# Moving element-wise work between GpSimd, VectorE and ScalarE in a two-layer trunk kernel: GpSimd keeps short powers and copies

## The chip, the cores and the metric

The kernel runs on one core of a Trainium2 chip. The metric is the device time of one execution in microseconds (us), here the median of three runs. Five engines take part, each with its own queue that it works off in order: TensorE (PE in the rows; PEld is its loading of weights), VectorE (DVE), ScalarE (ACT), GpSimd (POOL), and SyncE (SP), which here only issues transfers (DMA).

## The reference

A trunk of two layers runs on 512 new tokens and, with the same weights, on 8 single tokens of running sequences, so the kernel has 520 columns. Each layer is a mixer and a gated feed-forward network (FFN), each behind an RMS norm and with a residual sum. The first mixer multiplies chunks of 128 positions by a triangular matrix. The second is a gated delta rule, which is where most of the change lies. Cut to it:

```python
q, k, v = split(silu(short_conv(proj, w_conv)))      # 4 taps, per channel
q = l2norm(q) * DK ** -0.5;  k = l2norm(k)
beta = sigmoid(b_raw);  g = -exp(a_log) * softplus(a_raw + dt_bias)
gc = cumsum(g)                                        # within a chunk
decay = where(i >= j, exp(gc[i] - gc[j]), 0)
L = where(i > j, (k * beta) @ k.T * decay, 0)
Tm = inverse(I + L)
u, w = Tm @ (v * beta),  Tm @ (k * beta * exp(gc))
A = (q @ k.T) * decay
for each chunk:                                       # the scan
    v_new = u - w @ S
    o = (q * exp(gc)) @ S + A @ v_new
    S = S * exp(g_last) + (k * exp(g_last - gc)).T @ v_new
out = (rmsnorm(o) * silu(gate)) @ w_out
```

The kernel takes chunks of 128 positions in place of the reference's 64 for this rule: there are 8 heads of 128 and 4 chunks, 32 blocks of 128x128 in all.

## The kernel before, in words

Everything is kept with channels on the 128 partitions and the 520 columns along the free dimension, in two halves of 256 and 264 columns. Each projection is a row of tiles of weights, 128 output channels by 1024 input channels. A tile comes by DMA (`load_raw`), ScalarE rounds it to the type that TensorE multiplies fast (`split_w`, the CAST on L145), and VectorE or GpSimd takes the difference between the tile and its rounded form, its *rest* (L146). `mm3` then multiplies a half by three products (rounded by rounded, and rounded by rest both ways): 24 matmuls a half (L176), or 8 pairs of wider ones in the FFNs and the first mixer (L181, L182). A pool of three buffers each holds raw tiles and split tiles.

Stages, in the times of the profile: first mixer up to about 313 us, FFN 0 to 690, the delta layer to about 1103, FFN 1 to 1484, then the final norm. Within the delta layer: the end of FFN 0 and the norm in front of it (690 to 712); gates per position and the eight key tiles (712 to 815); the inverse of the 32x32 diagonal blocks on VectorE, beside which TensorE does projections (815 to 868); then the merging of these blocks, query and value tiles, the scan over chunks, and the output projection (868 to 1103).

A key tile (`key_tile`, L632) is a `conv_tile` (two `mm3`, scaled by L596; first tap on ScalarE L599, three taps on VectorE L601, the 8 single columns L602, Silu on ScalarE L603), and then two steps that `after(n, step)` puts off until n further `mm3` have been issued. `normalise` transposes the tile on TensorE (L642), squares it on ScalarE (L645), adds the epsilon (L646), takes `rsqrt`, and scales (L648). `back` transposes the result (L653) and makes the form scaled by decay (L655). TensorE works in order too, so a `back` that is not ready holds up all matmuls behind it.

`rsqrt` (L114) is nine small VectorE instructions (L121 to L130): a bit trick and two polynomial steps. The norms of the trunk (`Norm.add`, `Norm.factors`, `Norm.finish`) add squares into `sqacc` (L213, GpSimd unless told otherwise), sum over partitions on TensorE (L222), take `rsqrt`, and spread it over all partitions on TensorE (L244).

`decay` (L577) loads a row of cumulated decay for a head to all partitions, masks it on GpSimd (L580) and subtracts on VectorE (L581); one Exp over 16 blocks follows on ScalarE (L678). `lower` multiplies the key products by it (L669). `scan_step` (L817) does one chunk for four heads; it has two PSUM banks by turns, one of which (`po`) takes the output of the chunk.

The order on each engine comes from a scheduler with its own costs, except where `pin` and `after` fix it; so an edit can move instructions far from it.

Of the kernel before, what the change touches and what calls it, by code (L numbers as in the profile page):

```python
# [15 lines left out]
P = 128  # L16
# [5 lines left out]
H = 8  # L22
# [16 lines left out]
def trunk(  # L39
# [11 lines left out]
    wraw = ctx.enter_context(tc.tile_pool(name="wraw", bufs=3))  # L51
    wspl = ctx.enter_context(tc.tile_pool(name="wspl", bufs=3))
# [49 lines left out]
    G.memset(ones, 1.0)  # L102
    warm = cst.tile([P, 1], F32, name="warm")
# [90 lines left out]
    class Norm:  # L194
# [7 lines left out]
        def add(self, x, k, h, eng=None, split=False):  # L202
# [4 lines left out]
            else:  # L207
# [5 lines left out]
                (eng or G).tensor_tensor(a, a, t, ALU.add)  # L213
# [76 lines left out]
    def out_proj(w_out, k0, nk, act, x, xin=None, then=None, early=((), ()), halves=(0, 1), tail=2):  # L290
        ws, first = dict(early[0]), dict(early[1])
        order = [(j, h) for h in range(2) for j in ws] + [(n, h) for n in range(len(ws), 8 - tail) for h in range(2)]
        for j, h in order + [(j, h) for h in halves for j in range(8 - tail, 8)]:
            if j not in ws:
                ws[j] = weights(w_out[j][:, k0:k0 + nk, :], nk, G if then and j >= 6 else V)
# [63 lines left out]
    for u in range(8):  # L359
        ws = [weights(a_w_in[16 + 2 * u + j], eng=G if u == 1 else V) if u else w0[j] for j in range(2)]  # L360
# [77 lines left out]
    def ffn(layer, x, feed, then):  # L438
        w_in, w_out = f_w_in[layer], f_w_out[layer]
        hf, norm = feed.act, feed.norm  # L440
        for c0f, nk in ((0, 8), (8, 8), (16, 6)):
            mid = act_pair(3, "fm")
            for k in range(nk):
                wg = weights(w_in[c0f + k], eng=G if c0f + k == 0 else V)
# [7 lines left out]
                wu = weights(w_in[NF + c0f + k], eng=G if c0f + k == 0 else V)  # L452
# [21 lines left out]
    ffn(0, x, feed, feed_b)  # L474
    wide[0] = False
    hb, norm = feed_b.act, feed_b.norm


    gate_d = tc.dram_tile([P, H, TT], F32, name="gate_d")
    rows_d = tc.dram_tile([96, C], F32, name="rows_d")  # L480
    smp_d = tc.dram_tile([NS, 3, H], F32, name="smp_d")
    dl_d = tc.dram_tile([H, NS, P], F32, name="dl_d")

# [19 lines left out]

    order = [8 + i for i in range(8)] + [24 + i for i in range(5)] + [0, 1, 2, 3, 16, 17, 18, 19, 4, 5, 6, 7, 20, 21, 22, 23, 29, 30, 31]
    ready = {}
    POOL_LO = 17

    def stream(n):
        i = order.index(n)
        for j in order[i:i + 2]:  # L510
            if j not in ready:
                ready[j] = weights(b_w_in[j], eng=G if i < POOL_LO else V)
# [39 lines left out]
    V.tensor_copy(gc, ps[:, 0:32])  # L552
    egl = cst.tile([P, H, NCH], F32, name="egl")
# [23 lines left out]
    def decay(t, hd, keep, sign, base):  # L577
# [3 lines left out]
        V.tensor_tensor(t4, t4, gc[:, 4 * hd:4 * hd + 4, None].to_broadcast((P, 4, C)), ALU.subtract)  # L581
# [8 lines left out]
    def conv_tile(w, n, dst, y=None):  # L590
# [9 lines left out]
        for j in range(1, 4):  # L600
            V.scalar_tensor_tensor(y[:, :T], raw[:, j:j + T], wc[:, n, j:j + 1], y[:, :T], ALU.mult, ALU.add)  # L601
        V.scalar_tensor_tensor(y[:, T:TT], raw[:, 515:523], wc[:, n, 3:4], cs[:, n, :], ALU.mult, ALU.add)  # L602
# [29 lines left out]
    def key_tile(hd):  # L632
# [17 lines left out]
        def back():  # L650
# [4 lines left out]
            G.tensor_tensor(kt[:, q0:q0 + 4], kn, kdec[:, q0:q0 + 4, None].to_broadcast((P, NCH, C)), ALU.mult)  # L655
# [6 lines left out]
    def lower(hd):  # L662
# [5 lines left out]
        for c in range(NCH):  # L668
            V.scalar_tensor_tensor(L[:, q0 + c, :], ps[:, c * C:(c + 1) * C], beta[:, hd, c:c + 1], L[:, q0 + c, :], ALU.mult, ALU.mult)  # L669

    for hd in range(H):
# [4 lines left out]
        if hd in (2, 4):  # L676
            half = L[:, 8 * hd - 16:8 * hd]
            S.activation(half, half, AF.Exp, scale=-1.0)  # L678
# [95 lines left out]
    for gr in range(2):  # L774
        half = AT[:, 16 * gr:16 * gr + 16]
        S.activation(half, half, AF.Exp)

    def query_post(hd):
# [14 lines left out]
        G.tensor_tensor(qc[:, :T], qc[:, :T], er, ALU.mult)  # L793
# [23 lines left out]
    def scan_step(gr, c):  # L817
# [6 lines left out]
        if c:  # L824
# [9 lines left out]
            G.tensor_tensor(S4, S4, egl[:, hs, c:c + 1].to_broadcast((P, 4, P)), ALU.mult)  # L834
# [301 lines left out]
```

## Time and profile before

| | |
|---|---|
| time, median of 3 runs | 1494.62 us (1493.44 to 1494.76) |
| profiled execution | 1499.04 us; span of the trace 1497.3 us |
| granted TensorE clock, mean | 0.984 of full speed |
| busy in the span | PE 1442.0 us (96%), PEld 1359.5, DVE 888.3 (59%), ACT 584.4 (39%), POOL 436.9 (29%) |
| chain of work that ended last | PE 83%, DVE 11%, ACT 2%, issue 2%, DMA 1% |

The profiled execution lies 4.4 us above the median. Busy shares are means over the whole span: TensorE is busy almost throughout, and the stretches in which it is not are looked up by time. A wait of TensorE is shown with the instruction whose end released it.

### The profile page before, as it was taken

How to read it: one execution, taken by the hardware profiler on the slowest of the kernel's cores; microseconds unless marked ns; L12 is line 12 of the kernel's file. 1: busy time of each engine (PE TensorE's matmuls, PEld its weight loads, DVE VectorE, ACT ScalarE, POOL GpSimd, SP SyncE). 2: the span in 40 equal slices, each digit the busy share in tenths (PEclk: the TensorE clock that was granted, in tenths of full speed). 3: DMA queues.
4: the chain of work that ended last, by engine and by line, in shares of the span. 5: the costliest groups of instructions: out<-in, count | busy, mean ns of one | idle time of the engine just before them, and what ended most of it. 6: DMA issues, size and time to landing. Idle time of an engine off the chain costs nothing.

```text
span 1497.3 us, 27192 instructions
## 1 busy us (share of the span) xinstructions
PE 1442.0 (96%) x10752; PEld 1359.5 (91%) x10752; DVE 888.3 (59%) x1911; ACT 584.4 (39%) x1187; POOL 436.9 (29%) x468
## 2 busy tenths in 40 slices
PE   8999999999999999998788899999999999999997
PEld 7999999989999999997788888999999999999997
DVE  7657546664444444457787988676764454454454
ACT  6545324543313331333643255433533313331333
POOL 1113102333302320336444212311234412430333
PEclk9999999999999999999899999999999999999999
DMA  6222232322333333234312224334523553444332
GB/s 200 85 87 87 80 91 85 98 85 85 99 88 96 93 91 98 87 90 137 103 58 72 84 75 129 86 99 138 168 77 114 139 151 117 123 145 132 118 96 68
DMA packets 79359, 155.54 MB, mean 104 GB/s; under 512 B 10848, under 2 KB 41216, under 8 KB 79232
## 3 DMA queue, kind: packets, MB, share of 16 engines
q1 hardware_dynamic: 78944, 153.27, 33.9%
q8 instruction: 85, 1.39, 0.4%
q10 hardware_dynamic: 288, 0.52, 0.1%
q14 instruction: 42, 0.34, 0.1%
HBM read 142.18 MB, written 11.59 MB: 103 GB/s over the span
## 4 chain that ended last, share of the span: by engine, by line
PE 83%; DVE 11%; ACT 2%; issue 2%; DMA 1%; POOL 0%; SPq 0%; ACTq 0%; DVEq 0%; POOLq 0%
PE mm L176 42%; PE mm L181 22%; PE mm L182 11%; DVE r L601 1%; DVE inv L702 1%; PE ax L426 1%; PE ax L890 1%; DVE t L601 1%; DVE sc L701 1%; DMA raw<-in_a_w_in 1%; DVE rs_u L125 1%; PE ax L354 1%; DVE L L581 1%; DVE inv L694 1%; PE sx L842 1%
## 5 line engine op out<-in xcount | busy, mean ns | idle before, releaser
L145 ACT CAST wsp<-raw 128x1024 fp32r<-128x1024 f32 (+2 forms) x225 | 231.4, 1029 | 356.3 <-PE mm L176 298.5
L146 DVE TENSOR_TENSOR wsp<-raw,wsp 128x1024 fp32r<-128x1024 f32 (+2 forms) x193 | 235.2, 1219 | 87.8 <-ACT wsp L145 86.8
L176 PE MATMUL mm<-hf,wsp 128*128 128x264 f32 x2112 | 270.6, 284 | 0.0
L176 PEld LDWEIGHTS mm<-hf,wsp 128*128 128x128 f32 x2112 | 261.7, 188 | 3.7
L181 PE MATMUL mm<-hf,wsp 128*128 128x512 f32 x704 | 251.9, 397 | 0.0
L176 PE MATMUL mm<-hb,wsp 128*128 128x256 f32 (+1 forms) x1536 | 210.4, 293 | 6.8 <-DVE t L596 4.6
L176 PEld LDWEIGHTS mm<-hb,wsp 128*128 128x128 f32 x1536 | 196.2, 196 | 8.5 <-DVE t L596 3.8
L182 PE MATMUL mm<-hf,wsp 128*128 128x256 f32 x704 | 197.6, 281 | 0.0
L450 POOL TENSOR_TENSOR t<-t,rbc 128x256 f32<-128x256 f32 x88 | 95.1, 1081 | 314.1 <-ACT t L449 314.1
L181 PEld LDWEIGHTS mm<-hf,wsp 128*128 128x128 f32 x704 | 133.1, 189 | 27.9
L192 POOL TENSOR_TENSOR fm<-t,fm 128x256 fp32r<-128x256 f32 x88 | 95.9, 1090 | 147.6 <-ACT fm L191 147.6
L176 PE MATMUL mm<-fm,wsp 128*128 128x264 f32 x1056 | 135.2, 285 | 0.0
L182 PEld LDWEIGHTS mm<-hf,wsp 128*128 128x128 f32 x704 | 133.0, 189 | 0.0
L176 PEld LDWEIGHTS mm<-fm,wsp 128*128 128x128 f32 x1056 | 131.3, 190 | 1.6
L181 PE MATMUL mm<-fm,wsp 128*128 128x512 f32 x352 | 125.2, 395 | 0.0
L255 DVE TENSOR_TENSOR t<-mm,rbc 128x264 f32<-128x264 f32 (+1 forms) x160 | 68.2, 428 | 93.5 <-PE mm L176 90.4
L299 DVE TENSOR_TENSOR x<-mm,x 128x264 f32<-128x264 f32 (+1 forms) x128 | 54.5, 426 | 102.2 <-PE mm L176 73.3
L186 DVE TENSOR_TENSOR mm<-mm,t 128x256 f32<-128x256 f32 x120 | 51.7, 432 | 103.4 <-ACT t L185 103.2
L185 ACT COPY t<-mm 128x256 f32<-128x256 f32 x120 | 44.7, 373 | 142.6 <-PE mm L182 140.3
L181 PE MATMUL mm<-hn,wsp 128*128 128x512 f32 x256 | 96.1, 410 | 3.2 <-DVE hn L278 2.0
L176 PE MATMUL mm<-hn,wsp 128*128 128x264 f32 x768 | 99.2, 286 | 0.0
L182 PE MATMUL mm<-fm,wsp 128*128 128x256 f32 x352 | 98.6, 280 | 0.0
(331 smaller groups left out, 2233.3 us busy)
## 6 DMA issues: line engine op xcount, KB each, us to landing
raw<-in_f_w_in SPq DMA_DIRECT2D x88, 512.0 KB, 3.6
raw<-in_f_w_out SPq DMA_DIRECT2D x32, 512.0 KB, 3.6
raw<-in_b_w_in SPq DMA_DIRECT2D x32, 512.0 KB, 3.6
raw<-in_a_w_in SPq DMA_DIRECT2D x31, 512.0 KB, 3.6
raw<-in_a_w_out SPq DMA_DIRECT2D x16, 512.0 KB, 3.7
raw<-in_f_w_out SPq DMA_DIRECT2D x16, 384.0 KB, 3.1
L<-rows_d SPq DMA_DIRECT2D x16, 256.0 KB, 3.6
t<-in_st_delta SPq DMA_DIRECT2D x16, 256.0 KB, 3.2
```

The costliest lines, as they stand in the source:

```text
L145: S.copy(hi, r)
L146: (eng or V).tensor_tensor(w[:, 1, i:i + n, :], r, hi.bitcast(F32), ALU.subtract)
L176: PE.matmul(ps[:, :n], lhsT=w[:, a, k, :], rhs=act[:, b, k, c0:c0 + n], start=k + a + b == 0, stop=k == nk - 1 and a == 1)
L181: PE.matmul(ps.rearrange("p (b t) -> p b t", b=2), lhsT=w[:, 0, k, :], rhs=act[:, :, k, c0:c0 + n], start=k == 0, stop=last, skip_group_ch ...
L182: PE.matmul(ps[:, :n], lhsT=w[:, 1, k, :], rhs=act[:, 0, k, c0:c0 + n], start=False, stop=last, skip_group_check=True)
L185: S.copy(b, ps[:, n:])
L186: V.tensor_tensor(ps[:, :n], ps[:, :n], b, ALU.add)
L192: (eng or G).tensor_tensor(act[:, 1, k, c0:c0 + n], tmp, hi.bitcast(F32), ALU.subtract)
L255: V.tensor_tensor(t, ps[:, :n], self.r[:, c0:c0 + n], ALU.mult)
L299: V.tensor_tensor(dst, ps[:, :w], (xin(j)[:, c0:c0 + w] if xin else dst), ALU.add)
L450: G.tensor_tensor(s, s, norm.r[:, c0:c0 + nn], ALU.mult)
L601: V.scalar_tensor_tensor(y[:, :T], raw[:, j:j + T], wc[:, n, j:j + 1], y[:, :T], ALU.mult, ALU.add)
```

## The change

1. `rsqrt` of up to 4 columns becomes one GpSimd instruction, a `pow` with exponent -0.5. It serves the ten half norms of the trunk, the norm of `v` in the first mixer, the eight key tiles and the eight scan steps.
2. Rests of weights (L146) are all taken by VectorE; GpSimd had 28 tiles of 128x1024 and four of 128x768. The pools of raw and split tiles get a fourth buffer.
3. The norm's adds (L213) go from GpSimd to VectorE.
4. The subtraction in `decay` goes; in its place each of the 64 blocks has its own Exp on ScalarE with a bias per partition. The bias for `L` contains the logarithm of beta, so that `lower` is one product per head where it was four.
5. In `conv_tile` the 8 single columns ride on the last tap, after a ScalarE copy.
6. The scaling of keys (L655) and of the state (L834) go from GpSimd to ScalarE, in pieces of 128x128; the scaling of queries (L793) and of the scan's output (L859) go from GpSimd to VectorE. The scan's output is no longer copied from PSUM first (L850): squares and final product read PSUM.
7. Small loads and products for the running sequences' convolution (L484 to L502) are issued ahead of FFN 0.

```diff
-    wraw = ctx.enter_context(tc.tile_pool(name="wraw", bufs=3))
-    wspl = ctx.enter_context(tc.tile_pool(name="wspl", bufs=3))
+    wraw = ctx.enter_context(tc.tile_pool(name="wraw", bufs=4))
+    wspl = ctx.enter_context(tc.tile_pool(name="wspl", bufs=4))
...
     def rsqrt(s, n, p=P):
+        if n <= 4:
+            y = sm.tile([P, 4], F32, tag="rs_p", name=nm("rs_p"), bufs=4)[:p, :n]
+            G.tensor_tensor(y, s, mhalf[:p].to_broadcast((p, n)), ALU.pow)
+            return y
...
-                (eng or G).tensor_tensor(a, a, t, ALU.add)
+                (eng or V).tensor_tensor(a, a, t, ALU.add)
...
-                ws[j] = weights(w_out[j][:, k0:k0 + nk, :], nk, G if then and j >= 6 else V)
+                ws[j] = weights(w_out[j][:, k0:k0 + nk, :], nk)
...
-        ws = [weights(a_w_in[16 + 2 * u + j], eng=G if u == 1 else V) if u else w0[j] for j in range(2)]
+        ws = [weights(a_w_in[16 + 2 * u + j], eng=V) if u else w0[j] for j in range(2)]
...
-                ready[j] = weights(b_w_in[j], eng=G if i < POOL_LO else V)
+                ready[j] = weights(b_w_in[j], eng=V)
...
+    lnb = small([P, H, 5], "lnb")
+    S.activation(lnb, beta, AF.Ln)
     V.reciprocal(beta, beta)
+    V.tensor_scalar(lnb, lnb, -1.0, -BIG, ALU.mult, ALU.max)
...
+    gcb = cst.tile([P, 32], F32, name="gcb")
+    V.tensor_tensor(gcb.rearrange("p (h c) -> p h c", c=4), gc.rearrange("p (h c) -> p h c", c=4), lnb[:, :, 0:4], ALU.add)
+    ngc = cst.tile([P, 32], F32, name="ngc")
+    V.tensor_scalar(ngc, gc, -1.0, None, ALU.mult)
...
-        V.tensor_tensor(t4, t4, gc[:, 4 * hd:4 * hd + 4, None].to_broadcast((P, 4, C)), ALU.subtract)
+
+    def decay_exp(t, q0, sign, bias):
+        for q in range(q0, q0 + 16):
+            S.activation(t[:, q], t[:, q], AF.Exp, bias=bias[:, q:q + 1], scale=sign)
...
-        for j in range(1, 4):
-            V.scalar_tensor_tensor(y[:, :T], raw[:, j:j + T], wc[:, n, j:j + 1], y[:, :T], ALU.mult, ALU.add)
-        V.scalar_tensor_tensor(y[:, T:TT], raw[:, 515:523], wc[:, n, 3:4], cs[:, n, :], ALU.mult, ALU.add)
+        S.copy(y[:, T:TT], cs[:, n, :])
+        for j, m in ((1, T), (2, T), (3, TT)):
+            V.scalar_tensor_tensor(y[:, :m], raw[:, j:j + m], wc[:, n, j:j + 1], y[:, :m], ALU.mult, ALU.add)
...
-            G.tensor_tensor(kt[:, q0:q0 + 4], kn, kdec[:, q0:q0 + 4, None].to_broadcast((P, NCH, C)), ALU.mult)
+            for c in range(NCH):
+                S.activation(kt[:, q0 + c], kn[:, c], AF.Copy, scale=kdec[:, q0 + c:q0 + c + 1])
...
-        for c in range(NCH):
-            V.scalar_tensor_tensor(L[:, q0 + c, :], ps[:, c * C:(c + 1) * C], beta[:, hd, c:c + 1], L[:, q0 + c, :], ALU.mult, ALU.mult)
+        V.tensor_tensor(L[:, q0:q0 + 4], lanes(ps), L[:, q0:q0 + 4], ALU.mult)
...
-            half = L[:, 8 * hd - 16:8 * hd]
-            S.activation(half, half, AF.Exp, scale=-1.0)
+            decay_exp(L, 8 * hd - 16, -1.0, gcb)
...
-        half = AT[:, 16 * gr:16 * gr + 16]
-        S.activation(half, half, AF.Exp)
+        decay_exp(AT, 16 * gr, 1.0, ngc)
...
-        G.tensor_tensor(qc[:, :T], qc[:, :T], er, ALU.mult)
+        V.tensor_tensor(qc[:, :T], qc[:, :T], er, ALU.mult)
...
-            G.tensor_tensor(S4, S4, egl[:, hs, c:c + 1].to_broadcast((P, 4, P)), ALU.mult)
+            for i, hd in heads:
+                S.activation(Sd[:, hd], Sd[:, hd], AF.Copy, scale=egl[:, hd, c:c + 1])
...
-        S.copy(o_c, lanes(po))
...
-            S.activation(jk[:, i], o_c[:, i, :], AF.Square, accum_out=so[:, i:i + 1])
+            S.activation(jk[:, i], po[:, i * P:(i + 1) * P], AF.Square, accum_out=so[:, i:i + 1])
...
-        (V if gr and c == 3 else G).tensor_tensor(o_c, o_c, ro[:, :, None].to_broadcast((P, 4, P)), ALU.mult)
+        V.tensor_tensor(o_c, lanes(po), ro[:, :, None].to_broadcast((P, 4, P)), ALU.mult)
...
-        fin.add(x, k, h, G if h else V, split=True)
+        fin.add(x, k, h, V, split=True)
```

The order of instructions changes with it. The lines below carry each program's own line numbers; the changed program's are higher by 6 at the weights and by 14 to 16 in the delta layer (L146 becomes L152, L645 becomes L661, L648 becomes L664, L603 becomes L619, L701 and L702 become L716 and L717).

On VectorE, around the norm of the first key tile (`ssk` is the sum of squares, `rs_y` and `rs_p` the inverse root, `kns` the scaled tile), the program before has:

```order
L581 TENSOR_TENSOR L_7449<-L_7449,rows 128x512
L601 SCALAR_TENSOR_TENSOR r_7452<-t_941_7642,wc,r_7452 128x512
L581 TENSOR_TENSOR L_7449<-L_7449,rows 128x512
L596 TENSOR_TENSOR t_941_7642<-mm_7670,rbc_7284 128x264
L581 TENSOR_TENSOR L_7449<-L_7449,rows 128x512
L602 SCALAR_TENSOR_TENSOR r_7452<-t_941_7642,wc,cs 128x8
L592 MEMSET t_1000_8190 128x3
L646 TENSOR_SCALAR ssk_7595<-ssk_7595 128x4
L121 TENSOR_SCALAR rs_y_7606<-ssk_7595 128x4
L122 TENSOR_SCALAR rs_y_7606<-rs_y_7606 128x4
L124 SCALAR_TENSOR_TENSOR rs_u_7607<-rs_y_7606 128x4
L601 SCALAR_TENSOR_TENSOR r_7452<-t_941_7642,wc,r_7452 128x512
```

and the changed program, at the same norm:

```order
L612 TENSOR_TENSOR t_934_7575<-mm_7577,rbc_7249 128x256
L608 MEMSET t_988_8107 128x3
L612 TENSOR_TENSOR t_934_7575<-mm_7603,rbc_7249 128x264
L662 TENSOR_SCALAR ssk_7539<-ssk_7539 128x4
L664 TENSOR_TENSOR kns_7399<-ax_7538,rs_p_7550 128x512
L618 SCALAR_TENSOR_TENSOR r_7398<-t_934_7575,wc,r_7398 128x512
L612 TENSOR_TENSOR t_944_7691<-mm_7693,rbc_7249 128x256
L618 SCALAR_TENSOR_TENSOR r_7398<-t_934_7575,wc,r_7398 128x512
```

The subtractions and the nine steps of the root are gone, and the scaling stands directly behind the sum, with GpSimd's `pow` between the two; the taps that used to stand among the nine steps now stand behind the scaling.

On VectorE in the middle of the inverse (L701 and L702 make one step of it, each on what the last left), before:

```order
L701 TENSOR_TENSOR sc_1035_8492<-inv_8485 128x240
L702 TENSOR_TENSOR inv_8485<-inv_8485,sc_1035_8492 128x20x12
L701 TENSOR_TENSOR sc_1035_8492<-inv_8485 128x247
L702 TENSOR_TENSOR inv_8485<-inv_8485,sc_1035_8492 128x19x13
L701 TENSOR_TENSOR sc_1035_8492<-inv_8485 128x252
L596 TENSOR_TENSOR t_1070_8883<-mm_8885,rbc_7284 128x256
L702 TENSOR_TENSOR inv_8485<-inv_8485,sc_1035_8492 128x18x14
```

and changed:

```order
L716 TENSOR_TENSOR sc_1021_8388<-inv_8381 128x240
L717 TENSOR_TENSOR inv_8381<-inv_8381,sc_1021_8388 128x20x12
L261 TENSOR_TENSOR t_1040_8636<-mm_8611,rbc_7249 128x256
L716 TENSOR_TENSOR sc_1021_8388<-inv_8381 128x247
L717 TENSOR_TENSOR inv_8381<-inv_8381,sc_1021_8388 128x19x13
L152 TENSOR_TENSOR wsp_9114<-raw_9112,wsp_9114 128x1024
L716 TENSOR_TENSOR sc_1021_8388<-inv_8381 128x252
L717 TENSOR_TENSOR inv_8381<-inv_8381,sc_1021_8388 128x18x14
```

A rest of weights (L152) now stands between two steps; eight of them stand between the first step and the last, and before there was one, near the end.

On ScalarE at the first key tiles, before:

```order
L645 ACTIVATE t_936_7600,ssk_7595<-ax_7594 128x128
L599 ACTIVATE r_7452<-t_931_7541,wc 128x512
L645 ACTIVATE t_936_7600,ssk_7595<-ax_7594 128x128
L678 ACT_TABLE_LOAD
L678 ACTIVATE L_7449<-L_7449 128x2048
L645 ACTIVATE t_936_7600,ssk_7595<-ax_7594 128x128
L603 ACT_TABLE_LOAD
L603 ACTIVATE r_7452<-r_7452 128x520
```

and changed:

```order
L597 ACT_TABLE_LOAD
L597 ACTIVATE L_7395<-L_7395,gcb 128x128
L661 ACTIVATE t_930_7544,ssk_7539<-ax_7538 128x128
L597 ACTIVATE L_7395<-L_7395,gcb 128x128
L661 ACTIVATE t_930_7544,ssk_7539<-ax_7538 128x128
L619 ACT_TABLE_LOAD
L619 ACTIVATE r_7398<-r_7398 128x520
L661 ACTIVATE t_930_7544,ssk_7539<-ax_7538 128x128
L597 ACT_TABLE_LOAD
L597 ACTIVATE L_7395<-L_7395,gcb 128x128
```

The Exps are spread out between the squares and the Silus, and each change of function loads a table (ACT_TABLE_LOAD): 9 loads stand among the key tiles where there were 5, 6 at the query tiles where there were 4, 21 in the whole program where there were 15.

## Rows read from the trace of the kernel before

**Rows 1.** Busy time by stretch: length, each engine's busy us (instructions), granted clock, DMA.
```profile
690.00:712.00 22.00, 16.15 (x111) 15.06 (x110) 18.54 (x47) 5.86 (x12) 14.47 (x19) 0.91 0.33 109
712.00:775.00 63.00, 52.42 (x380) 50.82 (x380) 47.99 (x100) 36.52 (x73) 28.99 (x27) 0.87 0.27 87
775.00:815.00 40.00, 34.95 (x289) 33.93 (x290) 29.83 (x99) 16.19 (x50) 18.39 (x19) 1.00 0.21 68
815.00:868.00 53.00, 44.15 (x337) 43.34 (x336) 51.71 (x101) 14.33 (x18) 14.50 (x14) 0.94 0.27 81
868.00:1112.00 244.00, 236.07 (x2218) 226.93 (x2219) 181.80 (x511) 109.46 (x263) 60.00 (x74) 0.97 0.38 113
1112.00:1484.00 372.00, 372.00 (x2613) 348.80 (x2613) 181.09 (x345) 125.75 (x225) 120.30 (x112) 1.00 0.40 117
```

**Rows 2.** TensorE's waits over the whole run: total us, times, longest us.
```profile
PE ax L653 <- DVE kns L648: 15.0, 6, 6.3
PE ax L244 <- DVE t L238: 6.4, 4, 2.4
PE mm L176 <- DVE t L596: 4.6, 2, 3.6
PE sx L735 <- DVE r L712: 3.4, 1, 3.4
PE ax L222 <- DVE sqacc L213: 3.1, 2, 2.3
...
PE mm L182 <- POOL wsp L146: 2.0, 1, 2.0
```

**Rows 3.** GpSimd by line and shape, 676 to 868 us.
```profile
L146 POOL TENSOR_TENSOR wsp<-raw,wsp 128x1024 fp32r<-128x1024 f32 x18 | 43.9, 2438 | 37.8 <-ACT wsp L145 36.8 <-POOL sc L757 0.9
...
L635 POOL COPY kqs<-r 128x8 f32<-128x8 f32 x8 | 2.0, 251 | 16.9 <-ACT r L603 16.9
```

**Rows 4.** Instructions in order of time, norm of the first key tile: start, us, what.
```profile
742.85 2.52 POOL L146 TENSOR_TENSOR wsp<-raw,wsp 128x1024 fp32r<-128x1024 f32 x1 [1.80 <-ACT wsp L145]
743.08 2.31 DVE L125 TENSOR_TENSOR rs_u<-rs_u,ssk 128x4 f32<-128x4 f32 x1
...
748.50 1.12 PE L653 MATMUL ax<-ident,kns 128*128 128x128 f32 x4 [6.34 <-DVE kns L648]
```

**Rows 5.** The same view, last norm ahead of the delta layer.
```profile
707.56 2.38 DVE L122 TENSOR_SCALAR rs_y<-rs_y 128x3 int32<-128x3 int32 x1
```

**Rows 6.** VectorE by line and shape, 712 to 868 us: total us, mean ns.
```profile
L669 DVE SCALAR_TENSOR_TENSOR L<-ax,beta,L 128x128 f32<-128x128 f32 x32 | 9.6, 348 | 8.6 <-PE ax L667 8.6
L581 DVE TENSOR_TENSOR L<-L,rows 128x512 f32<-128x512 f32 x8 | 8.9, 1134 | 0.0
...
L125 DVE TENSOR_TENSOR rs_u<-rs_u,ssk 128x4 f32<-128x4 f32 x8 | 5.6, 701 | 0.1
L648 DVE TENSOR_TENSOR kns<-ax,rs_y 128x512 f32<-128x512 f32 x8 | 5.5, 692 | 0.3
...
L702 DVE TENSOR_TENSOR inv<-inv,sc 128x220 f32<-128x220 f32 x2 | 2.9, 1447 | 0.0
...
L126 DVE SCALAR_TENSOR_TENSOR rs_y<-rs_u,rs_y 128x4 f32<-128x4 f32 x8 | 1.3, 159 | 0.2
...
L146 DVE TENSOR_TENSOR wsp<-raw,wsp 128x1024 fp32r<-128x1024 f32 x1 | 1.2, 1219 | 0.0
...
L702 DVE TENSOR_TENSOR inv<-inv,sc 128x207 f32<-128x207 f32 x2 | 0.7, 370 | 0.0
```

**Rows 7.** ScalarE by line and shape, 712 to 775 us.
```profile
L645 ACT ACTIVATE t<-ax 128x128 f32<-128x128 f32 x16 | 4.4, 273 | 0.8 <-PE ax L642 0.5
...
L603 ACT ACT_TABLE_LOAD x3 | 3.8, 1283 | 0.1
L678 ACT ACTIVATE L<-L 128x2048 f32<-128x2048 f32 x2 | 3.8, 1915 | 0.0
...
L645 ACT ACTIVATION_READ_ACCUMULATOR t<-ax 128x1 f32 x16 | 3.1, 195 | 0.0
```

More of the change, by code (lines that the diff above doesn't have):

```diff
@@ L102, in trunk @@
     G.memset(ones, 1.0)
+    mhalf = cst.tile([P, 1], F32, name="mhalf")
+    G.memset(mhalf, -0.5)
     warm = cst.tile([P, 1], F32, name="warm")
@@ L443, in ffn @@
             for k in range(nk):
-                wg = weights(w_in[c0f + k], eng=G if c0f + k == 0 else V)
+                wg = weights(w_in[c0f + k])
                 sg = []
@@ L451, in ffn @@
                     sg.append(s)
-                wu = weights(w_in[NF + c0f + k], eng=G if c0f + k == 0 else V)
+                wu = weights(w_in[NF + c0f + k])
                 for h in range(2):
@@ L473, in trunk @@
     V.tensor_tensor(wba[:, 1, :, 0:16], rba, wba[:, 0, :, 0:16].bitcast(F32), ALU.subtract)
[L474 to L482, printed above, removed]
     wc = const_load(b_wc, (P, 24, 4), "wc")
@@ L502, in trunk @@
             G.tensor_tensor(cs, cs, t, ALU.add)
+    ffn(0, x, feed, feed_b)
+    wide[0] = False
+    hb, norm = feed_b.act, feed_b.norm
+    gate_d = tc.dram_tile([P, H, TT], F32, name="gate_d")
+    rows_d = tc.dram_tile([96, C], F32, name="rows_d")
+    smp_d = tc.dram_tile([NS, 3, H], F32, name="smp_d")
+    dl_d = tc.dram_tile([H, NS, P], F32, name="dl_d")
     order = [8 + i for i in range(8)] + [24 + i for i in range(5)] + [0, 1, 2, 3, 16, 17, 18, 19, 4, 5, 6, 7, 20, 21, 22, 23, 29, 30, 31]
     ready = {}
-    POOL_LO = 17
     def stream(n):
@@ L1114 @@
     }
-    nc = _bacc.Bacc("TRN2", target_bir_lowering=False, num_devices=1)
+    nc = _bacc.Bacc("TRN2", target_bir_lowering=False, num_devices=1, dynamic_dma_scratch_size=64)
     args = [nc.dram_tensor(f"in_{k}", a.shape, mybir.dt.from_np(a.dtype), kind="ExternalInput").ap() for k, a in arrays.items()]
```

## The prediction

> **What bounds the kernel now.** I read busy time by stretch first [rows 1]. From 1112 to 1484 us TensorE is busy for the whole of 372 us at full clock: nothing that the other engines do there can shorten it. Such a full stretch also gives the unit of TensorE's work: in 775 to 815 the clock is 1.00 and 289 matmuls take 34.95 us, 0.121 us each. The time to be won lies in the five stretches from 690 to 1112, where TensorE is idle for 5.85, 10.58, 5.05, 8.85 and 7.93 us, 38.3 in all. A second loss lies behind it: after such idle time the clock is granted at less than full, 0.87 in 712 to 775. Busy time times the missing share is 1.5, 6.8, 2.6 and 7.1 us in the four stretches below 1.00, 18 in all. With some 5 us at the program's start and at the norm after the first mixer, about 61 us is all that any edit to these parts can return.
>
> Who makes TensorE wait is read next, in its waits [rows 2]. The first five rows, 32.5 us, all end on VectorE: `back` for the scaled key (L653, 15.0), the spreading of a norm (L244, 6.4), a projection whose PSUM bank L596 had not emptied (4.6), the merging after the inverse (3.4), the norm's sum (3.1). The sixth, 2.0 at the start, ends on GpSimd's rest.
>
> Why VectorE is late is read from single instructions. At 742.85 GpSimd begins a rest of 2.52 us; VectorE's L125, four columns, begins at 743.08 and ends at the same instant as the rest, 2.31 us later; behind it `kns`, and TensorE's L653 has stood for 6.34 us when it starts [rows 4]. L126, as small, takes 159 ns, while L125's mean is 701 [rows 6]. In the inverse a step of 128x220 averages 1447 ns and one of 128x207 370, since one of the two of the first shape met a rest [rows 6]. 18 rests on GpSimd of 2438 ns, 43.9 us, stand between 676 and 868 [rows 3]. So two things are slow there: nine steps where a chain waits, and GpSimd instructions that hold VectorE off.
>
> **A rule beside this.** The Trainium skill, SBUF — State Buffer, section Who interferes with whom, says that a VectorE instruction with two SBUF inputs and a GpSimd instruction that reads SBUF exclude each other for the whole instruction; the 2.31 us agree. By the rule alone the change frees VectorE of every collision with a rest, and the short `pow` can still hold it off for its own length.
>
> **The change, stretch by stretch.**
>
> *690 to 712.* The path runs sum of squares, L222, root, L244. A `pow` replaces nine steps of which L122 alone took 2.38 us under GpSimd work [rows 5]; unhindered nine steps cost about 9 x 0.2 = 1.8 (159 ns and a gap). The norm's add goes to VectorE, at about the 0.4 us that L702 costs at 128x207. Of 5.85 us idle I take 3 back; between 0 and 5.85.
>
> *The price of `pow`.* No row shows one. Nearest is L635, a GpSimd copy of 128x8 at 251 ns; the far end is the longest GpSimd instruction shown, 2438 ns for 128x1024 [rows 3]. I take 0.5 us, near the small one, because start and end should outweigh four columns; what it costs at the other end stands with the rivals. In a key tile TensorE has 48 matmuls, 5.8 us, between `normalise` and `back`. Squares take 4 x (0.273 + 0.195) = 1.9 us [rows 7], with transposes, L646 and L648 some 3.3: about 2 us are left to hide `pow` and its two hand-overs.
>
> *712 to 775.* VectorE: 47.99 us [rows 1], less all eight subtractions 8.9, less half of the nine steps of eight tiles (5.6 for L125, at least 1.3 as L126 for each of the other eight: 16, half is 8), plus six rests at 1.219, 7.3 [rows 6]: 38. It stops being the bound. TensorE needs 380 x 0.121 = 46. ScalarE has 36.5, loses two wide Exps (3.8), gains 32 small ones at 0.273 as L645 (8.7; the wide pair is the lower end, so +4.9 at this price), 16 scalings at 0.273 (4.4; the work of L655), four table loads at 1.283 (5.1), and six copies of 8 columns at no more than 0.273 (I take 1.2 for all): 52 [rows 7]. The stretch cannot be shorter than 52 unless ScalarE's work slides into the next, which has 24 us of ScalarE idle. I take 55, so a gain of 8; between 0 and 17 (63 less 46).
>
> *The price of a change of table.* The rows have 1283 ns for a load. The Trainium skill, ScalarE: Activation LUTs, What ACT_TABLE_LOAD costs, adds a drain of about 1380 ns to it; by that ScalarE would have 9 x 1.38 = 12 us more among the key tiles, 64 in place of 52, which is an estimate from the page and would leave no gain in this stretch. No row of mine shows that drain, and the forecast goes by 1283.
>
> *775 to 815.* VectorE loses the other 8 us of roots and 9.6 - 8 x 0.692 = 4.1 in `lower` (L669 once per head, priced as L648, which also takes 512 columns from PSUM), and gains four rests, 4.9 [rows 6]. Idle 5.05, mostly L653: gain 3.5; between 0 and 5.
>
> *815 to 868.* VectorE is busy for 51.71 of 53: this is its own chain. Five rests less on GpSimd free four instructions of the inverse of about 2.1 us each (1447 x 2 less 2 x 370 for one pair), 8.4; but seven more rests at 1.219, 8.5, now stand between its steps: 51.8 as before. Gain 0; between -8.5, if the rests push the chain and what was hit is hit again by `pow` and fills, and 8.4, if the chain's own gaps take the rests up. What is won there is given back on the spot.
>
> *868 to 1112.* The wait behind the inverse (3.4) and the last norm (L244) fall partly; GpSimd no longer scales, and VectorE, 181.8 of 244, has room for the eight query scalings and seven output products that it gets. Two table loads more on ScalarE, 109 of 244, hide beside TensorE. The scan holds bank `po` longer: squares 1.9, three small steps, `pow`, product, about 4 us where one copy had freed it; TensorE has projections to do meanwhile in most steps, and where not it costs 1 to 2 us each time. Gain 4 of 7.9 idle; between -6 and 9.
>
> *Elsewhere.* The start: 2.0 us of wait on GpSimd's rest [rows 2], of which 1.2 for VectorE's stays, but clock comes back sooner; norms at 310 and at the end: 3.5 together; between 0 and 5. The fourth buffer and the early loads cost nothing: they stand before work that waits for TensorE, in stretches that TensorE fills.
>
> **Sum.** 3 + 8 + 3.5 + 0 + 4 + 3.5 = 22 us. The profiled execution takes 1499.04, its changed form 1477; the runs' median is 4.4 lower, so 1494.6 - 22 = 1472.6 is forecast.
>
> **Rivals.**
>
> *ScalarE becomes the bound among the key tiles.* Exps and tables stand between squares, as the order on ScalarE shows, so `normalise` ends later, and TensorE waits for ScalarE as it did for VectorE. For it: 52 of 63 us busy, and Silu behind each second load. Against: the six waits for `kns` of today end on VectorE, and ScalarE has idle time right after. Then 712 to 775 gives nothing, the clock stays low, and a third of the next stretch's gain goes too: 22 - 8 - 1.2 = 12.8 us, 1482.
>
> *The relief goes through whole.* With no wait longer than 1 us TensorE holds full clock, and 690 to 815 gives 24 rather than 14.5, the inverse 5, the later stretches 7, the others 4: 40 us, 1455. For it: the clock of 1.00 in 775 to 815 despite idle time. Against: ScalarE's sum.
>
> *`pow` is slow, and the kernel slower.* The scaling waits behind it in VectorE's queue, `back` in TensorE's, and behind that every matmul. At price p the eight key tiles lose 8(p - 2), eight scan steps as much through `po`, and some four half norms that lie bare 4(p - 1.8). The gain of 22 is used up where 20p - 39 = 22, at p = 3.1 us; at p = 3.6 the loss is 33, and the time 1494.6 + 11 = 1506. For it: no power shows in the trace. Against: small GpSimd work at 251 ns, and 2438 for 1024 columns, 256 times as many.
>
> *No change.* ScalarE binds the key tiles, which leaves 12.8 us, and the eight rests lengthen the inverse by all of their 9.8 without the collisions coming back: 3 us are left, 1492. For it: VectorE's 51.71 of 53 there. Against: the collisions have a cause in the rows, and it goes.
>
> **How the numbers follow.** My forecast (gain of 14 to 34) has 0.54; the whole relief 0.15, ScalarE as bound (gain 4 to 14) 0.16, no change 0.06, slow `pow` 0.09. A change within 0.2%, 3 us, is about what a measurement of this kernel can't tell from none. Faster 0.85, same 0.06, slower 0.09. The range of 8 in 10 runs from 1452 (most of the whole relief) to 1488 (most of ScalarE's case); by the bounds of the stretches alone the gain would lie between -15 and 50.
>
> **What would show it.** After: GpSimd has no L146 and no DVE instruction of 128x4 takes 2 us; the waits of L653 on L648 fall from 15.0 to under 4; the granted clock in the key stretch rises from 0.87 to 0.95 or more; the inverse stretch keeps about 52 us; `pow` rows read near 0.5 us. Wrong it would be if TensorE's first waits ended on ScalarE (L645, L603) or on GpSimd's `pow`, or if the inverse took over 55 us.

## The result

The changed kernel takes 1473.83 us (median of 4 runs, 1472.93 to 1474.44) against 1494.69 for the one before beside it (1493.44 to 1495.61): a ratio of 0.9861, with a 95% interval of 0.9843 to 0.9878, so 20.9 us faster. Forecast were 1472.6 us and a gain of 22. The profiled execution takes 1474.42 us with a span of 1472.7, which is 24.6 less than the span before; the account by stretch below is made against that.

The changed kernel's page, busy times and chain of work (its line numbers are its own):

```profile
PE 1437.3 (98%) x10752; PEld 1354.8 (92%) x10752; DVE 828.3 (56%) x1690; ACT 616.4 (42%) x1326; POOL 324.7 (22%) x399
...
PE 87%; DVE 6%; ACT 2%; POOL 1%; issue 1%; DMA 1%; SPq 0%; POOLq 0%; ACTq 0%; DVEq 0%
```

In the chain VectorE's share has gone from 11% to 6%. Busy time by stretch in the changed kernel, cut at the marks of the table further down (the columns are those of [rows 1]):

```profile
686.90:702.00 15.10, 14.61 (x117) 13.90 (x116) 10.48 (x33) 6.35 (x19) 5.97 (x13) 1.00 0.42 141
702.00:797.40 95.40, 83.30 (x626) 80.55 (x627) 50.01 (x97) 70.44 (x187) 22.38 (x35) 0.91 0.26 77
797.40:852.50 55.10, 49.93 (x413) 49.32 (x412) 54.03 (x113) 18.11 (x26) 3.21 (x10) 1.00 0.35 102
852.50:1046.50 194.00, 189.83 (x1837) 180.84 (x1838) 132.55 (x363) 98.93 (x284) 24.23 (x45) 0.97 0.39 112
1046.50:1089.40 42.90, 42.90 (x351) 42.12 (x349) 27.41 (x59) 20.86 (x40) 2.63 (x5) 1.00 0.41 124
1089.40:1461.70 372.30, 372.30 (x2614) 349.12 (x2614) 183.72 (x346) 125.23 (x226) 111.47 (x105) 1.00 0.40 115
```

and the key tiles, the inverse and the scan of the kernel before, cut at the same marks:

```profile
713.40:815.00 101.60, 85.97 (x664) 83.58 (x665) 77.82 (x198) 52.71 (x122) 47.38 (x46) 0.93 0.25 81
815.00:869.40 54.40, 44.15 (x337) 43.34 (x336) 53.07 (x103) 15.73 (x18) 14.50 (x14) 0.93 0.26 79
869.40:1066.00 196.60, 192.04 (x1874) 183.77 (x1874) 148.05 (x444) 87.67 (x224) 42.64 (x59) 0.98 0.38 113
```

And TensorE's waits over the whole run of the changed kernel (L669 is `back`, L653 before; L664 the scaled key, L648 before; L619 the Silu; L219 the norm's add; L727 the copy behind the inverse):

```profile
PE ax L669 <- DVE kns L664: 5.1, 4, 2.9
PE sx L750 <- DVE r L727: 3.5, 1, 3.5
PE ax L658 <- ACT r L619: 2.9, 2, 2.4
PE mm L182 <- ACT wsp L151: 2.1, 1, 2.1
...
PE ax L228 <- DVE sqacc L219: 1.5, 2, 1.0
```

Against [rows 2]: the wait for the scaled key has gone from 15.0 to 5.1 us, those for the spreading of a norm (6.4) are off this list, and two now end on ScalarE, 2.9 (L658 for the Silu, 0.7 before) and 2.1. The wait behind the inverse has stayed, 3.5 where it was 3.4.

All 9168 matmuls of the projections come in the same order in every program here, but for at most 28 places, and the small ones around them are known by line, so the same marks are found in each trace. Lengths in us, each from the start of one instruction to the start of the next named; the last four columns are experiments told below:

| stretch | before | changed | rests alone | rests back | rests twice | Exps grouped |
|---|---|---|---|---|---|---|
| start to the last tiles of FFN 0 | 690.1 | 686.9 | 685.4 | 690.9 | 686.7 | 686.7 |
| norm, to the first transpose of the gates | 23.3 | 15.1 | 17.7 | 23.8 | 24.0 | 15.1 |
| key tiles, to the inverse's first transpose | 101.6 | 95.4 | 90.4 | 101.0 | 105.4 | 87.4 |
| inverse, to the first matmul of the merging | 54.4 | 55.1 | 55.9 | 52.2 | 63.7 | 54.9 |
| merging, queries, values, scan | 196.6 | 194.0 | 190.7 | 201.8 | 191.0 | 193.5 |
| output projection and norm | 46.6 | 42.9 | 43.4 | 42.9 | 42.9 | 42.9 |
| FFN 1, to its last tiles | 371.4 | 372.3 | 371.4 | 373.1 | 372.7 | 373.1 |
| end | 13.3 | 11.0 | 13.3 | 11.0 | 11.0 | 11.0 |
| projection matmuls in norm, key tiles, inverse, scan | 94, 525, 335, 772 | 94, 487, 410, 735 | 104, 515, 411, 696 | 94, 487, 314, 831 | 94, 487, 410, 735 | 94, 509, 408, 715 |
| these four stretches together | 376.0 | 359.6 | 354.7 | 378.8 | 384.1 | 350.9 |

The stretches from the norm to the scan do not hold the same work in each column: the scheduler put different numbers of projection matmuls ahead of the marks. Only the four together do, 1726 matmuls in every column. A single row of two columns is compared safely where the counts are equal, as in the changed kernel and rests twice; elsewhere a matmul more or less is worth some 0.121 us, the prediction's estimate at full clock.

Two traces of the changed kernel agree within 1.6 us in each row but the scan's, where the second had 190.4 for 194.0 (356.5 for 359.6 in the four together); differences below 4 us in that row say nothing. Rows are rounded, so a difference of two can be off by 0.1.

The norm of the first key tile in the changed kernel, in order of time (engine, line, tile; [rows 4] shows the same place before):

```profile
722.30 0.20 ACT L661 ACTIVATION_READ_ACCUMULATOR t<-ax 128x1 f32 x1
722.51 1.28 ACT L619 ACT_TABLE_LOAD   x1
...
723.81 0.64 ACT L619 ACTIVATE r<-r 128x520 f32<-128x520 f32 x1
...
724.51 0.19 ACT L661 ACTIVATION_READ_ACCUMULATOR t<-ax 128x1 f32 x1
724.72 1.28 ACT L597 ACT_TABLE_LOAD   x1
...
726.01 0.40 ACT L597 ACTIVATE L<-L,gcb 128x128 f32<-128x128 f32 x1
...
726.70 0.17 DVE L662 TENSOR_SCALAR ssk<-ssk 128x4 f32<-128x4 f32 x1 [0.42 <-ACT t L661]
726.96 1.01 POOL L119 TENSOR_TENSOR rs_p<-ssk,mhalf 128x4 f32<-128x4 f32 x1 [2.26 <-DVE ssk L662]
...
728.00 0.69 DVE L664 TENSOR_TENSOR kns<-ax,rs_p 128x512 f32<-128x512 f32 x1 [1.13 <-POOL rs_p L119]
...
728.86 0.60 PE L669 MATMUL ax<-ident,kns 128*128 128x128 f32 x4
```

`pow` (L119) starts 0.09 us after the sum's end and takes 1.01; VectorE goes on 0.03 us after it. The rows also price a change of table: a square's accumulator is read until 722.50, the load takes 1.28, and the Silu begins at 723.81, 1.31 us in all. The drain of some 1.4 us that the Trainium skill adds (ScalarE: Activation LUTs, What ACT_TABLE_LOAD costs) is not in these rows; here the measurement decides.

All groups of `pow`, calls and mean ns behind the shapes:

```profile
L119 POOL TENSOR_TENSOR rs_p<-ssk,mhalf 128x4 f32<-128x4 f32 x8 | 9.4, 1171 | 27.1 <-DVE ssk L662 27.1
L119 POOL TENSOR_TENSOR rs_p<-nrm_s,mhalf 128x3 f32<-128x3 f32 x10 | 8.5, 854 | 162.7 <-DVE nrm_s L231 117.5 <-DVE nrm_s L233 44.1 <-DVE t L608 1.1
L119 POOL TENSOR_TENSOR rs_p<-so,mhalf 128x4 f32<-128x4 f32 x8 | 8.1, 1007 | 42.2 <-DVE so L870 42.2
```

### The profile page after: what moved, and what is told of

It reads as the page before. It is cut to its first block, busy times and chain, and to the rows that moved or that the text cites. A ratio compares the mean times of both kernels' runs of the same rounds, so it can differ in the third digit from the quotient of the medians.

```text
span 1472.7 us, 27006 instructions
## 1 busy us (share of the span) xinstructions
PE 1437.3 (98%) x10752; PEld 1354.8 (92%) x10752; DVE 828.3 (56%) x1690; ACT 616.4 (42%) x1326; POOL 324.7 (22%) x399
## 4 chain that ended last, share of the span: by engine, by line
PE 87%; DVE 6%; ACT 2%; POOL 1%; issue 1%; DMA 1%; SPq 0%; POOLq 0%; ACTq 0%; DVEq 0%
PE mm L182 45%; PE mm L187 22%; PE mm L188 11%; DVE wsp L152 1%; PE ax L432 1%; PE ax L904 1%; POOL rs_p L119 1%; DVE t L618 1%; DVE sc L716 1%; PE sx L857 1%; DVE inv L709 1%; DVE inv L717 1%; PE ax L684 1%; PE ax L360 1%; DMA raw<-in_a_w_in 0%
## 5 line engine op out<-in xcount | busy, mean ns | idle before, releaser
L151 ACT CAST wsp<-raw 128x1024 fp32r<-128x1024 f32 (+2 forms) x225 | 231.6, 1030 | 348.2 <-PE mm L182 305.8
L152 DVE TENSOR_TENSOR wsp<-raw,wsp 128x1024 fp32r<-128x1024 f32 (+2 forms) x225 | 270.8, 1204 | 97.2 <-ACT wsp L151 95.6
```

Of the source, the lines that this page charges most:

```text
L151: S.copy(hi, r)
L152: (eng or V).tensor_tensor(w[:, 1, i:i + n, :], r, hi.bitcast(F32), ALU.subtract)
```

## The experiments

Each run's time stands beside runs of the kernel before on the same chip, whose median there was 1497.0, 1498.1 or 1495.5 us; ratios are therefore what is compared.

**Rests back on GpSimd.** The changed kernel with the five choices of engine as before:

```diff
-                ready[j] = weights(b_w_in[j], eng=V)
+                ready[j] = weights(b_w_in[j], eng=G if i < 17 else V)
```

(and likewise at the first mixer's third and fourth tile, the first two of FFN, and the tiles that had GpSimd in the output projections).

> The changed kernel (1473.8 us) with the rests of weights given back to GpSimd as before; roots stay a GpSimd power, buffers stay four. Theory A (collisions are the larger half of the loss): 1483 to 1490, GpSimd rows of about 2.4 us back in the delta layer, and VectorE instructions in the inverse of over 2 us again. Rival B (the root's nine steps were what was hit, so without them rests on GpSimd hurt little): 1473 to 1478. A third effect is new: the power would stand behind a 2.4 us rest in GpSimd's queue, which belongs to neither and shows as TensorE waits for the scaled key of up to 3 us.

Measured: 1494.88 us, ratio 0.9993 (0.9981 to 1.0004). All of the gain is gone, more than the upper end of theory A. Rival B is out. The third effect came once: the first key tile's power starts 1.58 us after its sum, the other seven 0.08. In the inverse the hit instructions are back (VectorE by shape, 815 to 868 us):

```profile
L717 DVE TENSOR_TENSOR inv<-inv,sc 128x255 f32<-128x255 f32 x2 | 2.9, 1465 | 0.1
...
L716 DVE TENSOR_TENSOR sc<-inv 128x207 f32<-128x207 f32 x2 | 2.8, 1402 | 0.1
```

Each is a pair of some 0.4 and some 2.5 us. The norm ahead of the delta layer is hit too, now at the two small diagonal products (L244) that follow the power:

```profile
700.99 0.85 POOL L119 TENSOR_TENSOR rs_p<-nrm_s,mhalf 128x3 f32<-128x3 f32 x1 [6.36 <-DVE nrm_s L231]
701.88 3.52 DVE L244 TENSOR_SCALAR t<-ident,rs_p 128x128 f32<-128x128 f32 x2 [0.96 <-POOL rs_p L119]
...
702.00 2.39 POOL L152 TENSOR_TENSOR wsp<-raw,wsp 128x1024 fp32r<-128x1024 f32 x1
```

**Rests alone.** The kernel before with those five choices set to VectorE, nothing else; three buffers, nine-step roots, wide Exps.

> The kernel before (1494.7 us) with all rests on VectorE and nothing else. Theory A (collisions are the larger half): 1480 to 1487. Rival (VectorE, at 51.7 of 53 us in the inverse, pays as much as it gets back): 1491 to 1496.

Measured: 1470.05 us, ratio 0.9814 (0.9794 to 0.9833), a gain of 28 us, more than theory A's range. One part of seven gives the whole gain, and VectorE hardly pays for it: the inverse takes 55.9 us for 54.4. The order of instructions changes with the edit, though: 1030 of the 1726 projection matmuls, for 954 before, now stand ahead of the merging. The next run holds the order fixed. VectorE's rows from 700 to 860 us:

```profile
L146 DVE TENSOR_TENSOR wsp<-raw,wsp 128x1024 fp32r<-128x1024 f32 x19 | 23.4, 1233 | 1.8 <-ACT wsp L145 1.8
...
L581 DVE TENSOR_TENSOR L<-L,rows 128x512 f32<-128x512 f32 x8 | 6.3, 792 | 2.3 <-POOL L L580 2.3
...
L125 DVE TENSOR_TENSOR rs_u<-rs_u,ssk 128x4 f32<-128x4 f32 x8 | 1.7, 208 | 0.1
```

L125, one of the nine steps, is at 208 ns where it was 701, and the subtraction in `decay` at 792 where it was 1134 [rows 6], with neither step removed. The key tiles' windows row, with the granted clock in the seventh place:

```profile
703.10:793.50 90.40, 81.26 (x655) 78.69 (x655) 72.03 (x209) 52.60 (x122) 26.30 (x39) 0.98 0.31 91
```

**Rests computed twice.** Do rests on GpSimd cost because VectorE is held off, or because TensorE gets them later? In the changed kernel, VectorE still makes every rest that is used, and GpSimd makes 18 again for nobody (with three raw buffers in place of four):

```diff
-                ready[j] = weights(b_w_in[j], eng=V)
+                raw = load_raw(b_w_in[j], KD)
+                ready[j] = split_w(raw, KD, V)
+                if i < 17:
+                    G.tensor_tensor(junk, raw, ready[j][:, 0].bitcast(F32), ALU.subtract)
```

> The changed kernel, with GpSimd computing each of the 18 rests of the delta layer a second time into a scratch tile that nobody reads; VectorE's rests are still the ones used. So nothing of the result waits for GpSimd, but its reads of SBUF are back. Giving the rests back whole had cost 21 us. If collisions are the cause: 10 to 20 us slower than the changed kernel, with VectorE instructions of 2 us and more in the inverse, though part of this is the power standing behind a 2.4 us instruction. If the cause was that TensorE waits for the slower rest itself: 0 to 4 us. (Raw buffers are three here, which by the run with three buffers is worth nothing.)

Measured: 1499.07 us, ratio 1.0020 (1.0011 to 1.0028), against 0.9835 for the changed kernel on this chip: 27 us for work that no result waits for, more than the range of the collisions. The order is not the cause: in the two traces TensorE's 10752 instructions stand in the same order, and VectorE's in all but 9 places of 1690. In the middle of the inverse (L720 and L721 are its steps, L521 the idle rest):

```profile
839.64 0.40 DVE L720 TENSOR_TENSOR sc<-inv 128x231 f32<-128x231 f32 x1
840.08 0.40 DVE L721 TENSOR_TENSOR inv<-inv,sc 128x231 f32<-128x231 f32 x1
840.11 2.64 POOL L521 TENSOR_TENSOR junk<-raw,wsp 128x1024 f32<-128x1024 f32 x1 [3.72 <-issue]
840.51 2.51 DVE L720 TENSOR_TENSOR sc<-inv 128x240 f32<-128x240 f32 x1
843.05 0.41 DVE L721 TENSOR_TENSOR inv<-inv,sc 128x240 f32<-128x240 f32 x1
...
845.33 2.66 POOL L521 TENSOR_TENSOR junk<-raw,wsp 128x1024 f32<-128x1024 f32 x1 [0.71 <-POOL r L639]
845.63 2.64 DVE L720 TENSOR_TENSOR sc<-inv 128x252 f32<-128x252 f32 x1
```

A step of 0.40 us becomes one of 2.51 when it starts 0.40 us behind GpSimd, and ends 0.27 us after GpSimd does. The stretch of the inverse, where no power stands, has grown from 55.1 to 63.7 us, with VectorE busy for 62.64 of it:

```profile
816.10:879.80 63.70, 53.74 (x413) 52.49 (x411) 62.64 (x113) 17.79 (x26) 15.25 (x15) 0.95 0.30 88
```

So the collisions by themselves are worth 8.6 us there: the same 113 instructions of VectorE take 54.03 us in the changed kernel, and four held steps of L720 make up the difference. In the norm and key stretches (+8.9 and +10.0) the idle rests could also hold raw tiles longer and stand ahead of the power in GpSimd's queue. The second did not come about: each power there starts 0.08 or 0.09 us after its sum, as in the changed kernel. VectorE's 97 instructions among the key tiles take 63.44 us for 50.01. The queue of the weights' loads waited for an idle rest twice, 4.5 us in all; whether that reached TensorE was not separated.

**Roots back on VectorE.** The changed kernel with

```diff
-        if n <= 4:
+        if n <= 0:
```

> The changed kernel with the root of nine VectorE steps again, nothing else. An unhindered root takes 1.8 us against 1.0 for the power and two hand-overs. Theory A (collisions): 1474 to 1478, since without rests on GpSimd the steps run at 0.16 to 0.2 us each. Rival B (the root itself was the path): 1480 to 1488, waits for the scaled key above 10 us in total.

Measured: 1473.28 us, ratio 0.9841 (0.9823 to 0.9858), the same as the changed kernel. Rival B is out again: not the nine steps, but what stood on them. In its trace the nine steps do cost 2.2 us at the end and 0.5 at the norm behind the output projection, and the stretches from the norm to the scan give it back (354.5 for 359.6 and 356.5).

**Power alone**, in the kernel before.

> The kernel before with the power in place of the short roots and nothing else. Theory A: the power stands behind rests of 2.4 us in GpSimd's queue as the root's steps stood blocked by them, so little is won: 1490 to 1497. Rival B (the root's nine steps are the path): 1482 to 1488.

Measured: 1494.57 us, ratio 0.9981 (0.9968 to 0.9994), some 3 us. By stretch its trace gains where the root lies bare: 2.3 us at the end (10.9 long, where the traces without the power have 13.2 or 13.3), 3.1 at the norm behind the output projection and 1.8 at the one ahead of the delta layer. From the key tiles to the scan it loses 2.9 (355.6 for 352.7), for a reason that was not looked for. It is not theory A's: in all eight key tiles the power starts 0.08 or 0.09 us after the sum, so it did not stand behind rests.

**Three buffers.**

> The changed kernel with three raw and three split buffers again. My prediction gave the fourth buffer no worth: 1473 to 1475. Rival: the fourth buffer feeds TensorE where rests wait among VectorE's own work (inverse, norms), and without it the time is 1477 or more, with waits of projections on rests or casts.

Measured: 1473.89 us, ratio 0.9850 (0.9832 to 0.9868): no worth, as forecast.

**Norm's adds back on GpSimd** (`eng or G`).

> The changed kernel with the norms' adds of squares on GpSimd again. Theory N (the norm ahead of the delta layer, which gave 8 us where 3 were forecast, gained by the adds and by the freed VectorE together): 1476 to 1480, with TensorE waiting 1 to 2 us more for the sum of squares at each norm. Rival: the adds are hidden beside TensorE, 1473 to 1475.

Measured: 1473.23 us, ratio 0.9835 (0.9816 to 0.9855). The rival holds; in its trace the norm stretch is 16.6 us for 15.1, which the measurement of the whole does not resolve.

**Wide Exp and subtraction.** The changed kernel with the decay as before, but beta's logarithm kept in the subtracted sum, so `lower` stays one product a head:

```diff
+        off = gcb if sign > 0 else gc
+        V.tensor_tensor(t4, t4, off[:, 4 * hd:4 * hd + 4, None].to_broadcast((P, 4, C)), ALU.subtract)
...
-        for q in range(q0, q0 + 16):
-            S.activation(t[:, q], t[:, q], AF.Exp, bias=bias[:, q:q + 1], scale=sign)
+        half = t[:, q0:q0 + 16]
+        S.activation(half, half, AF.Exp, scale=sign)
```

> The changed kernel with the decay's subtraction on VectorE again (of the sum that contains beta's logarithm) and one Exp over 16 blocks: 15 table loads in place of 21, 16 subtractions of about 0.7 us more on VectorE, 64 Exps fewer on ScalarE. Theory S (ScalarE, with Exps and table loads, held the key tiles to a gain of 6 us where 11.5 were forecast): 1468 to 1472. Rival V (VectorE would again be late, as before): 1478 to 1484.

Measured: 1466.69 us, ratio 0.9799 (0.9782 to 0.9816). Faster than the changed kernel, by more than theory S forecast: S holds in its direction, this part of the change costs time.

**Exps grouped.** What in it costs, the Exps' own time or where they stand? The 64 small Exps are kept in program order and so stand mostly in groups of 14 to 16:

```diff
-            S.activation(t[:, q], t[:, q], AF.Exp, bias=bias[:, q:q + 1], scale=sign)
+            pin(S.activation(t[:, q], t[:, q], AF.Exp, bias=bias[:, q:q + 1], scale=sign))
```

> The changed kernel with its 64 small Exps kept in program order, so that they stand mostly in groups of 14 to 16: 17 table loads in place of 21, no subtraction on VectorE, the same Exps. If the changes of table and the Exps spread between the squares were what cost 7 us: 1467 to 1470 (ratio 0.980 to 0.983). If the Exps' own time was (64 pieces in place of 4): no change, 0.984 to 0.987.

Measured: 1466.32 us, ratio 0.9802 (0.9785 to 0.9819); on the same chip the changed kernel itself was at 1471.86, so 5.5 us. ScalarE by line among the key tiles, in the changed kernel:

```profile
L672 ACT ACTIVATE r<-kns,kdec 128x128 f32<-128x128 f32 x32 | 10.7, 394 | 8.0 <-DVE kns L664 8.0
L597 ACT ACTIVATE L<-L,gcb 128x128 f32<-128x128 f32 x32 | 10.6, 395 | 5.4 <-POOL L L593 5.4
...
L619 ACT ACT_TABLE_LOAD x5 | 6.4, 1283 | 0.1
...
L597 ACT ACT_TABLE_LOAD x4 | 5.1, 1283 | 0.1
```

and with grouped Exps, followed by the stretch's row of busy times:

```profile
L597 ACT ACTIVATE L<-L,gcb 128x128 f32<-128x128 f32 x32 | 9.8, 389 | 0.0
...
L619 ACT ACT_TABLE_LOAD x3 | 3.8, 1283 | 0.1
L597 ACT ACT_TABLE_LOAD x2 | 2.6, 1283 | 0.0
```

```profile
701.80:789.20 87.40, 79.92 (x649) 77.90 (x649) 51.94 (x99) 66.07 (x184) 25.24 (x38) 0.98 0.30 93
```

The same 32 Exps take 9.8 and 10.6 us; loads for Silu and Exp fell from nine to five, 5.1 us of ScalarE. The stretch is 8.0 us shorter, with 22 projection matmuls more in it, and the clock 0.98 where the changed kernel had 0.91. It is the order, not the Exps' number. Three things in the order were not separated: the loads, the squares waiting between Exps, and the 5.4 us for which ScalarE stood idle ahead of Exps until GpSimd's mask (L593) was done, which are gone with grouping.

**Keys' scaling back on GpSimd.**

```diff
-            for c in range(NCH):
-                S.activation(kt[:, q0 + c], kn[:, c], AF.Copy, scale=kdec[:, q0 + c:q0 + c + 1])
+            G.tensor_tensor(kt[:, q0:q0 + 4], kn, kdec[:, q0:q0 + 4, None].to_broadcast((P, NCH, C)), ALU.mult)
```

> The changed kernel with the scaling of keys (eight products of 128x512) on GpSimd again. Theory S (ScalarE is short of time among the key tiles): 1470 to 1474, slightly faster, as 32 ScalarE pieces of about 0.3 us go. Rival: GpSimd's 1.1 us products collide with VectorE and delay the next power: 1476 to 1480.

Measured: 1469.41 us, ratio 0.9809 (0.9791 to 0.9828); the key stretch is 90.5 us for 95.4. Its interval overlaps that of the changed kernel's second measurement (0.9820 to 0.9851), so the total shows the gain less surely than the stretch. ScalarE was short there.

**Both together**, wide Exps and keys on GpSimd.

> Both edits that were faster, together: wide Exps with subtraction on VectorE, and the scaling of keys on GpSimd. If both worked by relieving ScalarE among the key tiles, the second adds little: 1464 to 1468 (ratio 0.978 to 0.981). If they are separate, 1461 to 1464 (ratio 0.975 to 0.978).

Measured: 1466.74 us, ratio 0.9804 (0.9790 to 0.9818). The second adds nothing to the first: both relieve the same engine in the same stretch, which is 88.3 us long with wide Exps alone and 88.2 with both.

**The changed kernel again**, beside the last three.

> The changed kernel itself, so that it stands beside the next three on one chip: ratio to before 0.983 to 0.987.

Measured: 1471.86 us, ratio 0.9835 (0.9820 to 0.9851).

The best version here is the changed kernel with grouped or wide Exps, about 1466.5 us, 0.980 of the time before.

## Why the prediction was right, by its own steps

The total was right, and the likeliest case was the one that came; but its terms were off in both directions, so that their sum fits is luck in part, and one of its two causes was not one.

- *690 to 712*, forecast 3: the table gives 23.3 - 15.1 = 8.2. I had counted idle time alone; the clock there came back from 0.91 to 1.00 as well, and the stretch goes on past 712 to the gates. Rests alone give 5.6 of it, with ten projection matmuls more in the stretch.
- *712 to 815*, forecast 8 + 3.5: measured 6.2, and 38 projection matmuls, by 0.121 each some 4.6 us, have left the stretch; TensorE's idle time in it fell from 15.63 to 12.10 only. The rival of ScalarE as the bound came half true. ScalarE is busy for 70.44 of 95.4 us, where VectorE has 50.01; two waits of TensorE, 2.9 and 2.1 us, now end on it; the clock is 0.91, where I wanted 0.95 to see the step right. ScalarE's sum was near: 52 and the 16.19 of the second stretch are 68, for 70.44 measured, and its pieces of 128x128, priced at 273, follow each other by 0.30 us. What I left out is their order, which cost 8.0 us by the run with grouped Exps.
- *815 to 868*, forecast 0: measured -0.7. For VectorE's chain the account by its two halves was right. Rests computed twice have both the eight rests and the collisions, 63.7; the changed kernel has the rests and no collisions, 55.1. So the collisions are worth 8.6, where I had 8.4. (Rests back, 52.2, hold 19 VectorE instructions and 96 projection matmuls fewer than the changed kernel and show no price.) For TensorE the 0 was wrong: beside a chain of the same length it now does 410 projection matmuls in place of 335, some 9 us of work at 0.121, is idle for 5.17 us in place of 10.25, and has the clock at 1.00 for 0.93. Not all that was won there was given back on the spot.
- *868 to 1112*, forecast 4: measured 2.6 + 3.8 = 6.4, the second with the norm behind the output projection. The 2.6 is less than the 37 projection matmuls that left the scan (some 4.5) and lies within the noise of that row. The longer hold of the bank `po` shows as 1.6 us of waits in two pieces (L847 on L873).
- *Elsewhere*, forecast 3.5: 3.2 up to the last tiles of FFN 0, -0.9 in FFN 1, 2.3 at the end, 4.5 together before rounding.

The sum is 8.2 + 6.2 - 0.7 + 6.4 + 4.5 = 24.6 of span, or 20.9 by the medians. Of this 16.4 lie in the four stretches that hold the same work only together (19.4 by the second trace).

Of the signs that were set down, three did not come: the wait for the scaled key fell to 5.1 and not under 4, the clock of the key stretch is below 0.95, and the power takes twice 0.5. One sign of being wrong came by a hair, the inverse at 55.1 for 55, though by the same marks it had 54.4 before.

The step that failed in kind is the one about causes: "two things are slow there: nine steps where a chain waits, and GpSimd instructions that hold VectorE off". Only the second was, for the most part. Putting the nine steps back costs nothing in the whole (some 3 us at the bare norms, given back elsewhere), and the power alone brings 3 us; the steps' 16 us that I took off VectorE's sum came off an engine that, once free of rests, was no bound. The price of `pow` was off by two (0.5 against 1.01 us), below the 3.1 at which it would have mattered, since 2 us were there to hide it. And I read a sum of seven parts as if all helped, where one gave 28 us alone and the decay's part took 5 to 7 back.

The rule of the Trainium skill that I set beside the rows (SBUF — State Buffer, Who interferes with whom) turned out to be the larger part of the case: VectorE's steps with two SBUF inputs are held until GpSimd's instruction ends, in 2.51 for 0.40 us above. The order on ScalarE is a part that it does not reach. A collision that is left in the changed kernel stands at the end of the program, where a norm's add of 0.4 us meets GpSimd's final products:

```profile
1460.90 4.42 POOL L1029 TENSOR_TENSOR xg<-xg,rbc 128x792 f32<-128x792 f32 x2 [2.37 <-ACT rbc L253]
...
1461.48 2.12 DVE L219 TENSOR_TENSOR sqacc<-sqacc,t 128x256 f32<-128x256 f32 x1
```

## What to carry to other kernels

Before shortening a slow chain of small instructions, look at what runs beside its slowest members: here 18 wide GpSimd instructions in a scheduled stretch cost 27 us though no result waited for them, and moving them onto the engine that seemed full was nearly free, since part of its busy time had been time in which it was held. Work that is shared out anew to an idle engine is priced by its queue, not by its busy time: small Exps among Silus and squares cost the key tiles 8 us by their order alone, and the whole 5.5. Before two traces are compared by stretch, count the work between the marks: here 75 matmuls had moved into a stretch whose length stayed. When several edits come together, run each alone and each undone; a right total says little about the parts.

## What the runs showed of the hardware that was not expected

A GpSimd `pow` takes 0.854 us for 128x3 and 1.007 us for 128x4 in most calls; from these two alone, an estimate is 0.15 us for each column and about 0.4 fixed. VectorE's diagonal product L244, with one tile input and a scalar per partition, is held as well: the longest with rests back has 3316 ns, where the median is 285, and its record spans a GpSimd rest and two fills. Which of them holds it was not separated. ScalarE's pieces of 128x128 from SBUF to SBUF have records of 395 ns but follow each other by 0.30 (eight in 2.43 us at 735.55 in the changed kernel).
